# Attention sums from unnormalised exponentials, scaled once per head pair, with prob turned by transposes

## The chip, the cores and the metric

The kernel runs on one core of a Trainium2 chip. Its time is the device time of one execution in microseconds; here there is one core, so it is that core's. Times of single instructions come from one profiled execution.

## The reference, cut to what matters

Two layers, each of a gated feed-forward block, a mixer of three kinds of heads, and another feed-forward block, on 512 tokens of width 1024, all in float32. The change is in the softmax attention of the mixer: 4 heads with shared keys and values (A) and 6 heads whose three dilated windows act as one softmax with a bias added to the scores (B).

```python
def dense_gqa(q, k, v):
    ...
        s = jnp.einsum('bqhgd,bkhd->bhgqk', qi, k).astype(F32) * (D ** -0.5)
        p = jax.nn.softmax(s, axis=-1)
        return jnp.einsum('bhgqk,bkhd->bqhgd', p.astype(v.dtype), v)

def dilated_branch(q, k, v, rel_bias, window, dil):
    ...
    lse = jax.nn.logsumexp(s, axis=-1)
    p = jnp.exp(s - lse[..., None])
    o = jnp.einsum('brnhqk,brnkhd->brnqhd', p.astype(v.dtype), vw)
    ...
```

What is needed of a head is softmax(scores) times v: the exponentials weighted with v, divided by the sum of the exponentials of that query row.

## The kernel before, in words

Activations are kept with features on the 128 partitions and the 512 tokens along the free axis. Large matmuls are made in three products of rounded parts (`mm3`, lines 216 to 218). `body` runs, for each of two layers, `ffn`, `mixer`, `ffn`.

Within `mixer` the attention stage is `Mixer.attention` (line 919), a generator of 20 units: 5 head pairs (`tile_`, 0 and 1 are the A heads, 2 to 4 the B heads) times 4 blocks `t` of 128 query tokens. Between units `mixer` puts the other work of the stage: joining the blocks of a triangular solve (lines 699 and 705, fed by DMAs of X and Y), eight steps of a scan over chunks (`delta_scan`, lines 733 to 780, at the units in `SCAN_AT`), and its end (`delta_finish`, line 1028). After the stage, `project_out` multiplies the eight tiles of `self.mix` with the output weights, tile 4, the last head pair, last (`OUT_ORDER`).

A unit has two halves. `scores` makes the scores of the two heads of the pair (TensorE, lines 954 and 955, into `psc`), their row maximum (VectorE, line 962, or line 966 with the bias), the exponential `prob` with its row sum (ScalarE, lines 963 and 968, the sum through `accum_out`), then on VectorE the reciprocal of the sum (line 970) and `share`, the identity scaled row by row with it (line 971). `weigh`, one unit later (`AHEAD = 1`), turns each 128x128 block of prob with a matmul whose right side is `share` (line 981, four to a PSUM bank `ppt`), so that turning and normalising are one matmul; ScalarE copies the bank to SBUF (`pth`, line 984); line 988 multiplies with v and accumulates into `pav`, the lower head in partitions 0 to 63 and the upper in 64 to 127, over four key blocks. At the fourth block, `pav` holds the pair's 512 tokens and is split into `mxh` (ScalarE, line 993) and `mxl` (VectorE, line 994), the two rounded parts that `project_out` reads.

PSUM in this stage: `psc` has two banks (tag s), `ppt` and the blocks of queries and keys that `load` turns (`pqk`, line 887, a transpose with the identity) share two (tag t), and `pav` has one (tag v). The order of the instructions on each engine is made by a planner (`schedule_with_timeline_sim=True`) from its own estimate of times; each engine then runs its list in order.

Of the kernel before, what the change touches and what calls it, by code (L numbers as in the profile page):

```python
# [9 lines left out]
F32 = mybir.dt.float32  # L10
# [3 lines left out]
AF = mybir.ActivationFunctionType  # L14
ALU = mybir.AluOpType
# [4 lines left out]
P = 128  # L20
T = 512
# [3 lines left out]
NT = T // P  # L25
NL = 2
FGROUPS = [8, 7, 7]
AHEAD = 1
# [351 lines left out]
class Mixer:  # L380
# [495 lines left out]
    low, high = slice(0, 64), slice(64, 128)  # L876
# [42 lines left out]
    def attention(self, ap, pp):  # L919
        k, nc, c = self.k, self.nc, self.c  # L920
        ident = c["ident"]
        self.mix, self.exps = [None] * KD, []
        low, high = self.low, self.high
        ops = {0: self.first}

        def load(i):
            bank = lambda: pp.tile([P, T], F32, name="pqk", tag="t", bufs=2)
            home = self.homes[i % 2]
            if i == 1:
                ops[i] = (self.queries(home, self.turned(bank(), self.qkv[0], i), 0.125), *ops[0][1:])  # L930
            elif i < 5:
                g = self.qkv[i - 1]
                ops[i] = (self.queries(home, self.turned(bank(), g, 0), self.gq8),
                          self.keys((i - 1) % 2, self.turned(bank(), g, 1), self.nbk), g[:, :, 256:384])

        state = {}

        def scores(tile_, t):
            ps = [pp.tile([P, T], F32, name="psc", tag="s", bufs=2) for _ in range(2)]
            if t == 0:  # L940
                state["pv"] = pp.tile([P, T], F32, name="pav", tag="v")
                state["bias"] = []
                if tile_ >= 2:
                    for h in (2 * tile_ - 4, 2 * tile_ - 3):
                        bias = ap.tile([P, NWIN], F32, name="bias", bufs=BIAS_BUFS)
                        src = k.line[h:h + 1, 0:P * 2 * T].rearrange("o (p n) -> (o p) n", n=2 * T)
                        nc.sync.dma_start(out=bias, in_=src[:, P - 1:P - 1 + NWIN])
                        state["bias"].append(bias)
            if t == LOAD_AT:
                load(tile_ + 1)  # L950
            tk = slice(t * P, t * P + P)
            q, (kh, kl), v = ops[tile_]
            for par in range(2):
                nc.tensor.matmul(out=ps[par], lhsT=q[par][:, tk], rhs=kh[:, par], start=True, stop=False)
                nc.tensor.matmul(out=ps[par], lhsT=q[par][:, tk], rhs=kl[:, par], start=False, stop=True)
            probs = []
            for par in range(2):
                pb = ap.tile([P, T], F32, name="prob", bufs=2 * AHEAD + 2)
                row = ap.tile([P, 2], F32, name="row", bufs=2 * AHEAD + 2)
                nm, sm = row[:, 0:1], row[:, 1:2]  # L960
                if tile_ < 2:
                    nc.vector.tensor_reduce(out=nm, in_=ps[par], axis=AX, op=ALU.max, negate=True)
                    self.exps.append(nc.scalar.activation(out=pb, in_=ps[par], func=AF.Exp, bias=nm, accum_out=sm))
                else:
                    o = T - P - t * P
                    nc.vector.tensor_tensor_reduce(out=pb, in0=ps[par], in1=state["bias"][par][:, o:o + T], scale=1.0,
                                                   scalar=3e38, op0=ALU.add, op1=ALU.min, accum_out=nm)
                    nc.scalar.activation(out=pb, in_=pb, func=AF.Exp, scale=-1.0, bias=nm, accum_out=sm)
                share = ap.tile([P, P], F32, name="share", bufs=2 * AHEAD + 2)
                nc.vector.reciprocal(out=sm, in_=sm)  # L970
                nc.vector.tensor_scalar(out=share, in0=ident, scalar1=sm, scalar2=None, op0=ALU.mult)
                probs.append((pb, share))
            return probs, state["pv"], v, tile_, t

        def weigh(probs, pv, v, tile_, t):
            tk = slice(t * P, t * P + P)
            turns = []
            for pb, share in probs:
                pt = pp.tile([P, T], F32, name="ppt", tag="t", bufs=2)
                for kt in range(NT):  # L980
                    nc.tensor.matmul(out=pt[:, kt * P:kt * P + P], lhsT=pb[:, kt * P:kt * P + P], rhs=share,  # L981
                                     start=True, stop=True)
                full = ap.tile([P, T], F32, name="pth", bufs=4)
                nc.scalar.activation(out=full, in_=pt, func=AF.Copy)
                turns.append(full)
            for kt in range(NT):
                for hb, full in zip((low, high), turns):
                    nc.tensor.matmul(out=pv[hb, tk], lhsT=v[:, kt, hb], rhs=full[:, kt * P:kt * P + P],  # L988
                                     start=kt == 0, stop=kt == NT - 1)
            if t == NT - 1:  # L990
                hi = k.xp.tile([P, T], F32R, name="mxh", tag=f"xh{tile_}")
                lo = k.xp.tile([P, T], F32R, name="mxl", tag=f"xl{tile_}")
                nc.scalar.activation(out=hi, in_=pv, func=AF.Copy)
                nc.vector.tensor_tensor(out=lo, in0=pv, in1=hi, op=ALU.subtract)
                self.mix[tile_] = hi, lo

        pending = []
        for unit in range(5 * NT):
            pending.append(scores(*divmod(unit, NT)))
            if len(pending) > AHEAD:  # L1000
                weigh(*pending.pop(0))
            yield unit
        for u in pending:
            weigh(*u)
# [136 lines left out]
```

## Time and profile before

| | |
|---|---|
| median of 3 runs | 2210.26 us (2210.14 to 2210.66) |
| profiled execution | 2210.73 us, of which the span of the trace is 2208.9 us |
| TensorE matmul busy | 2174.3 us, 98% |
| VectorE busy | 1130.1 us, 51% |
| ScalarE busy | 782.1 us, 35% |
| line 981, matmuls | 640 records, mean 284 ns, busy 91.8 us |
| line 988, matmuls | 640 records, mean 285 ns, busy 59.2 us |

PE stands for TensorE, PEld for its weight loads, DVE for VectorE, ACT for ScalarE, POOL for GpSimd. Matmuls are pipelined: one lasts about 275 ns from start to end, but the next starts long before that, so busy times of TensorE overlap and what a matmul costs is read from how soon the next one starts, or from the chain of waits, where each piece begins where the one before it ends. The attention stage lies at about 561 to 695 us in layer 0 and 1655 to 1790 us in layer 1.

### The profile page before, as it was taken

The numbers are of one execution on the slowest core, as the hardware profiler recorded it, in microseconds if no ns is written. First come the engines' busy times: TensorE is split into PE (matmuls) and PEld (weight loads), VectorE is DVE, ScalarE is ACT, GpSimd is POOL, SyncE is SP. The second block draws the span as 40 slices with busy tenths as digits, with TensorE's granted clock in tenths as the row PEclk, the third lists the DMA queues.
The fourth block names the chain that finished last, engine by engine and source line by source line (L and its number), as shares of the span: only waits on it lengthen the run. The fifth ranks groups of instructions, "written<-read, shape, count | busy, mean of one in ns | idle before, by whom it ended". The sixth has DMA issues, their size and how long they took to land.

```text
span 2208.9 us, 31208 instructions
## 1 busy us (share of the span) xinstructions
PE 2174.3 (98%) x12868; PEld 1754.8 (79%) x12868; DVE 1130.1 (51%) x1867; ACT 782.1 (35%) x1147; POOL 320.0 (14%) x298
## 2 busy tenths in 40 slices
PE   7999999999999999999999999999999999999999
PEld 5888887779787888888788888877797878888887
DVE  5333344688776543433443333447796755333343
ACT  4222223534754322222332222235446534222221
POOL 3101012120111210101211010123001121101010
PEclk9999999999999999999999999999999999999999
DMA  5432323233302223232323323232322032332323
GB/s 174 128 96 95 96 93 114 92 83 93 85 28 96 94 91 94 95 96 95 89 93 95 96 92 99 90 122 77 93 88 72 28 115 86 96 96 93 98 93 98
DMA packets 93526, 206.88 MB, mean 94 GB/s; under 512 B 38625, under 2 KB 39137, under 8 KB 93384
## 3 DMA queue, kind: packets, MB, share of 16 engines
q1 hardware_dynamic: 91616, 199.98, 29.3%
q10 hardware_dynamic: 1768, 4.91, 0.8%
q8 instruction: 101, 1.65, 0.3%
q14 instruction: 41, 0.34, 0.0%
HBM read 193.83 MB, written 14.18 MB: 94 GB/s over the span
## 4 chain that ended last, share of the span: by engine, by line
PE 91%; DVE 3%; ACT 2%; DMA 2%; issue 1%; POOL 1%; SPq 0%; ACTq 0%; POOLq 0%; DVEq 0%
PE pg L218 15%; PE pg L216 15%; PE pg L217 15%; PE pd L218 7%; PE pd L216 7%; PE pd L217 7%; PE ppt L981 4%; PE pav L988 2%; PE pgr L807 2%; PE pgr L808 2%; PE pgr L806 2%; PE pc L216 1%; PE pc L218 1%; PE pc L217 1%; PE pwo L218 1%; PE pwo L216 1%
## 5 line engine op out<-in xcount | busy, mean ns | idle before, releaser
L210 ACT ACTIVATE whi<-wraw 128x1024 fp32r<-128x1024 f32 (+3 forms) x344 | 351.0, 1022 | 1224.4 <-PE pg L217 659.8
L216 PE MATMUL pg<-xh,whi 128*128 128x512 f32 x1408 | 558.0, 397 | 8.2 <-ACT xh L236 8.1
L217 PE MATMUL pg<-xl,whi 128*128 128x512 f32 x1408 | 558.4, 397 | 2.3 <-DVE xl L237 2.3
L218 PE MATMUL pg<-xh,wlo 128*128 128x512 f32 x1408 | 557.8, 396 | 0.8 <-DVE wlo L211 0.8
L211 DVE TENSOR_TENSOR wlo<-wraw,whi 128x1024 fp32r<-128x1024 f32 (+3 forms) x344 | 408.0, 1186 | 72.5 <-ACT whi L210 63.6
L216 PEld LDWEIGHTS pg<-xh,whi 128*128 128x128 f32 x1408 | 265.2, 188 | 73.0 <-ACT xh L236 8.1
L217 PEld LDWEIGHTS pg<-xl,whi 128*128 128x128 f32 x1408 | 265.1, 188 | 68.0 <-DVE xl L237 4.7
L296 POOL TENSOR_TENSOR s<-s,rstd 128x512 f32<-128x512 f32 x88 | 152.2, 1731 | 1147.1 <-ACT s L295 1147.1
L218 PEld LDWEIGHTS pg<-xh,wlo 128*128 128x128 f32 x1408 | 265.2, 188 | 65.2 <-DVE wlo L211 1.9
L218 PE MATMUL pd<-hh,wlo 128*128 128x512 f32 x704 | 278.8, 396 | 0.9 <-DVE wlo L211 0.9
L216 PE MATMUL pd<-hh,whi 128*128 128x512 f32 x704 | 278.5, 396 | 0.0
L217 PE MATMUL pd<-hl,whi 128*128 128x512 f32 x704 | 278.4, 395 | 0.0
L310 DVE SCALAR_TENSOR_TENSOR x<-pd,x 128x512 f32<-128x512 f32 x96 | 66.4, 691 | 284.7 <-PE pd L218 284.7
L298 DVE TENSOR_TENSOR h<-pg,s 128x512 f32<-128x512 f32 x88 | 60.9, 692 | 288.0 <-PE pg L218 281.5
L294 DVE TENSOR_TENSOR s<-pg,rstd 128x512 f32<-128x512 f32 x88 | 60.6, 691 | 230.5 <-PE pg L218 230.4
L218 PEld LDWEIGHTS pd<-hh,wlo 128*128 128x128 f32 x704 | 132.3, 188 | 34.0 <-DVE wlo L211 2.2
L217 PEld LDWEIGHTS pd<-hl,whi 128*128 128x128 f32 x704 | 132.4, 188 | 31.9
L216 PEld LDWEIGHTS pd<-hh,whi 128*128 128x128 f32 x704 | 132.4, 188 | 31.7
L981 PE MATMUL ppt<-share,prob 128*128 128x128 f32 x640 | 91.8, 284 | 3.8 <-DVE qs L897 3.8
L981 PEld LDWEIGHTS ppt<-share,prob 128*128 128x128 f32 x640 | 80.1, 191 | 15.3 <-issue 5.8
L807 PE MATMUL pgr<-wlo,xh 128*128 128x384 f32 (+1 forms) x256 | 90.1, 352 | 0.2
L808 PE MATMUL pgr<-whi,xl 128*128 128x384 f32 (+1 forms) x256 | 90.0, 353 | 0.0
(248 smaller groups left out, 2506.4 us busy)
## 6 DMA issues: line engine op xcount, KB each, us to landing
wraw<-in_gu_dram SPq DMA_DIRECT2D x176, 512.0 KB, 3.6
wraw<-in_wd_dram SPq DMA_DIRECT2D x64, 448.0 KB, 3.3
wraw<-in_wd_dram SPq DMA_DIRECT2D x32, 512.0 KB, 3.6
wraw<-in_w_c_dram SPq DMA_DIRECT2D x24, 512.0 KB, 3.7
wraw<-in_w_gb_dram SPq DMA_DIRECT2D x24, 384.0 KB, 3.0
wraw<-in_w_o_dram SPq DMA_DIRECT2D x14, 512.0 KB, 4.4
bias<-line SPq DMA_DIRECT2D x12, 448.0 KB, 5.4
saved<-x SPq DMA_DIRECT2D x16, 256.0 KB, 2.0
```

Source lines behind the costliest of these rows:

```text
L210: nc.scalar.activation(out=hi, in_=raw, func=AF.Copy)
L211: nc.vector.tensor_tensor(out=lo, in0=raw, in1=hi, op=ALU.subtract)
L216: nc.tensor.matmul(out=out, lhsT=w[0], rhs=x[0], start=first, stop=False)
L217: nc.tensor.matmul(out=out, lhsT=w[0], rhs=x[1], start=False, stop=False)
L218: nc.tensor.matmul(out=out, lhsT=w[1], rhs=x[0], start=False, stop=last)
L294: nc.vector.tensor_tensor(out=s, in0=p, in1=n["rstd"], op=ALU.mult)
L296: nc.gpsimd.tensor_tensor(out=s, in0=s, in1=n["rstd"], op=ALU.mult)
L298: nc.vector.tensor_tensor(out=h, in0=pp[1], in1=s, op=ALU.mult)
L310: nc.vector.scalar_tensor_tensor(out=self.x[dm], in0=p, scalar=0.5, in1=self.x[dm], op0=ALU.mult, op1=ALU.add)
L807: nc.tensor.matmul(out=o, lhsT=xh[:, tk], rhs=lo[:, wc], start=False, stop=False)
L808: mm = nc.tensor.matmul(out=o, lhsT=xl[:, tk], rhs=hi[:, wc], start=False, stop=kk == KD - 1)
L981: nc.tensor.matmul(out=pt[:, kt * P:kt * P + P], lhsT=pb[:, kt * P:kt * P + P], rhs=share, start=True, stop=True)
```

## The change

The exponentials are no longer normalised before they are weighted. Each row's sum goes into a column of a new tile `sums` (one per head pair, 4 blocks by 2 heads); the reciprocal and the scaled identity of each unit are gone. Line 981's matmul becomes a transpose with the identity, as line 887 has it. At the fourth block of a head pair one reciprocal is taken of all eight columns, and eight matmuls spread it: each multiplies one column, repeated 64 times as the left side, with the identity, which gives 64 equal rows of 128 tokens; the lower head's into partitions 0 to 63 and the upper head's into 64 to 127 of a bank of tag t. ScalarE copies that bank to SBUF (`share`, now 128x512), VectorE multiplies `pav` with it in place, and the split into `mxh` and `mxl` reads the product from SBUF instead of `pav`.

```diff
--- before.py
+++ after.py
@@ -939,6 +939,7 @@
             ps = [pp.tile([P, T], F32, name="psc", tag="s", bufs=2) for _ in range(2)]
             if t == 0:
                 state["pv"] = pp.tile([P, T], F32, name="pav", tag="v")
+                state["sums"] = ap.tile([P, NT, 2], F32, name="sums", bufs=2)
                 state["bias"] = []
                 if tile_ >= 2:
                     for h in (2 * tile_ - 4, 2 * tile_ - 3):
@@ -956,8 +957,8 @@
             probs = []
             for par in range(2):
                 pb = ap.tile([P, T], F32, name="prob", bufs=2 * AHEAD + 2)
-                row = ap.tile([P, 2], F32, name="row", bufs=2 * AHEAD + 2)
-                nm, sm = row[:, 0:1], row[:, 1:2]
+                nm = ap.tile([P, 1], F32, name="row", bufs=2 * AHEAD + 2)
+                sm = state["sums"][:, t, par:par + 1]
                 if tile_ < 2:
                     nc.vector.tensor_reduce(out=nm, in_=ps[par], axis=AX, op=ALU.max, negate=True)
                     self.exps.append(nc.scalar.activation(out=pb, in_=ps[par], func=AF.Exp, bias=nm, accum_out=sm))
@@ -966,20 +967,16 @@
                     nc.vector.tensor_tensor_reduce(out=pb, in0=ps[par], in1=state["bias"][par][:, o:o + T], scale=1.0,
                                                    scalar=3e38, op0=ALU.add, op1=ALU.min, accum_out=nm)
                     nc.scalar.activation(out=pb, in_=pb, func=AF.Exp, scale=-1.0, bias=nm, accum_out=sm)
-                share = ap.tile([P, P], F32, name="share", bufs=2 * AHEAD + 2)
-                nc.vector.reciprocal(out=sm, in_=sm)
-                nc.vector.tensor_scalar(out=share, in0=ident, scalar1=sm, scalar2=None, op0=ALU.mult)
-                probs.append((pb, share))
-            return probs, state["pv"], v, tile_, t
-
-        def weigh(probs, pv, v, tile_, t):
+                probs.append(pb)
+            return probs, state["pv"], state["sums"], v, tile_, t
+
+        def weigh(probs, pv, sums, v, tile_, t):
             tk = slice(t * P, t * P + P)
             turns = []
-            for pb, share in probs:
+            for pb in probs:
                 pt = pp.tile([P, T], F32, name="ppt", tag="t", bufs=2)
                 for kt in range(NT):
-                    nc.tensor.matmul(out=pt[:, kt * P:kt * P + P], lhsT=pb[:, kt * P:kt * P + P], rhs=share,
-                                     start=True, stop=True)
+                    nc.tensor.transpose(out=pt[:, kt * P:kt * P + P], in_=pb[:, kt * P:kt * P + P], identity=ident)
                 full = ap.tile([P, T], F32, name="pth", bufs=4)
                 nc.scalar.activation(out=full, in_=pt, func=AF.Copy)
                 turns.append(full)
@@ -990,8 +987,17 @@
             if t == NT - 1:
                 hi = k.xp.tile([P, T], F32R, name="mxh", tag=f"xh{tile_}")
                 lo = k.xp.tile([P, T], F32R, name="mxl", tag=f"xl{tile_}")
-                nc.scalar.activation(out=hi, in_=pv, func=AF.Copy)
-                nc.vector.tensor_tensor(out=lo, in0=pv, in1=hi, op=ALU.subtract)
+                nc.vector.reciprocal(out=sums, in_=sums)
+                spread = pp.tile([P, T], F32, name="pshare", tag="t", bufs=2)
+                for u in range(NT):
+                    for par, hb in enumerate((low, high)):
+                        nc.tensor.matmul(out=spread[hb, u * P:u * P + P], lhsT=sums[:, u, par:par + 1].to_broadcast([P, 64]),
+                                         rhs=ident, start=True, stop=True)
+                share = ap.tile([P, T], F32, name="share")
+                nc.scalar.activation(out=share, in_=spread, func=AF.Copy)
+                nc.vector.tensor_tensor(out=share, in0=pv, in1=share, op=ALU.mult)
+                nc.scalar.activation(out=hi, in_=share, func=AF.Copy)
+                nc.vector.tensor_tensor(out=lo, in0=share, in1=hi, op=ALU.subtract)
                 self.mix[tile_] = hi, lo
 
         pending = []
```

## Rows read from the trace of the kernel before

**Rows 1.** The page: span; busy time by engine; the chain that ended last, by line

```profile
span 2208.9 us, 31208 instructions
PE 2174.3 (98%) x12868; PEld 1754.8 (79%) x12868; DVE 1130.1 (51%) x1867; ACT 782.1 (35%) x1147; POOL 320.0 (14%) x298
...
PE pg L218 15%; PE pg L216 15%; PE pg L217 15%; PE pd L218 7%; PE pd L216 7%; PE pd L217 7%; PE ppt L981 4%; PE pav L988 2%; PE pgr L807 2%; PE pgr L808 2%; PE pgr L806 2%; PE pc L216 1%; PE pc L218 1%; PE pc L217 1%; PE pwo L218 1%; PE pwo L216 1%
```

**Rows 2.** Stretch: us; busy us of PE, PEld, DVE, ACT, POOL; clock, DMA, GB/s

```profile
600.00:640.00 40.00, 39.23 (x631) 32.42 (x631) 31.69 (x77) 24.16 (x47) 2.83 (x4) 1.00 0.08 25
```

**Rows 3.** Chain of waits, 600 to 640 us (start us, us, what, records)

```profile
by line: PE ppt L981 33.6%; PE pav L988 18.2%; PE prr L746 8.4%; PE psc L954 8.4%; PE pkq L733 6.4%; PE psc L955 6.2%; PE pS L756 6.2%; PE po L769 5.5%; PE pqk L887 2.9%; DVE qs L897 1.9%; ACT qs L896 1.7%; issue 0.5%
...
608.09 1.09 PE ppt L981 x8
...
612.14 0.89 PE ppt L981 x8
...
619.51 1.02 PE pav L988 x14
620.52 0.86 PE ppt L981 x6
...
622.25 0.64 PE ppt L981 x4
622.89 0.36 PE pav L988 x2
623.25 0.58 PE pqk L887 x4
```

**Rows 4.** Groups by line and form (xcount, busy us, mean ns, idle before)

```profile
L981 PE MATMUL ppt<-share,prob 128*128 128x128 f32 x640 | 91.8, 284 | 3.8 <-DVE qs L897 3.8
...
L887 PE MATMUL pqk<-consts,qkv 128*128 128x128 f32 x56 | 10.4, 299 | 0.0
...
L971 DVE TENSOR_SCALAR share<-consts,row 128x128 f32<-128x128 f32 x80 | 28.0, 350 | 1.9
...
L970 DVE RECIPROCAL row<-row 128x1 f32<-128x1 f32 x80 | 12.7, 159 | 16.3 <-ACT prob L963 7.8 <-ACT prob L968 7.0
```

**Rows 5.** Busy time by stretch, line 981 alone (matmuls, weight loads)

```profile
600.00:640.00 40.00, 14.87 (x102) 12.82 (x102) 1.00 0.08 25
```

**Rows 6.** Chain of waits, 640 to 693 us

```profile
681.05 1.02 PE pav L988 x16
...
689.36 0.44 PE pot L1028 x4
```

**Rows 7.** Timeline at two head pairs' ends (start us, us, instruction, idle before, releaser)

```profile
614.27 1.09 PE L988 MATMUL pav<-pth,qkv 128*64 128x128 f32 x14
...
620.56 0.60 ACT L993 ACTIVATE mxh<-pav 128x512 fp32r<-128x512 f32 x1 [1.45 <-PE pav L988]
...
621.19 0.69 DVE L994 TENSOR_TENSOR mxl<-pav,mxh 128x512 fp32r<-128x512 f32 x1 [0.18 <-ACT mxh L993]
...
675.41 0.60 ACT L993 ACTIVATE mxh<-pav 128x512 fp32r<-128x512 f32 x1 [0.98 <-PE pav L988]
...
678.15 0.68 DVE L994 TENSOR_TENSOR mxl<-pav,mxh 128x512 fp32r<-128x512 f32 x1
```

**Rows 8.** Timeline at the last head pair of layer 0

```profile
695.86 0.68 DVE L994 TENSOR_TENSOR mxl<-pav,mxh 128x512 fp32r<-128x512 f32 x1
...
697.95 0.39 PE L216 MATMUL pwo<-mxh,wohi 128*128 128x512 f32 x1
```

**Rows 9.** Timeline at the start of the attention stage of layer 0

```profile
569.25 0.50 PE L954 MATMUL psc<-kh,qs 128*128 128x512 f32 x1 [2.15 <-ACT prob L963]
...
570.97 1.65 PEld L699 LDWEIGHTS pp<-X,Y 32*32 32x32 f32 x100 [0.27 <-DMA X<-s]
...
572.68 1.77 PE L988 MATMUL pav<-pth,qkv 128*64 128x128 f32 x14
```

**Rows 10.** Busy time by stretch, one us (columns as in rows 2)

```profile
571.00:572.00 1.00, 1.00 (x67) 1.00 (x70) 1.00 (x3) 1.00 (x3) 0.00 (x0) 0.50 0.01 4
```

## Prediction

> **What bounds the kernel now.** I read the page first. TensorE is busy for 2174.3 of the 2208.9 us, and of the chain that ended last 4% is line 981, the turning of prob; nothing but TensorE's lines stands high in it [rows 1]. A busy share says little where matmuls overlap, so I then read the stretch that the change touches, the attention stage (about 561 to 695 us, and again about 1655 to 1790 us). Between 600 and 640 us TensorE is busy 39.23 of 40 us, VectorE 31.69, ScalarE 24.16, at a granted clock of 1.00 [rows 2]. Third, the chain of waits of that stretch, whose pieces follow one another on TensorE: its summary gives 33.6% to line 981, 18.2% to the weighted sums of line 988, and to VectorE and ScalarE less than 2% each [rows 3]. So the stage is as long as its TensorE work. What is taken from that work shortens it, until something else is late.
>
> **Turning prob.** The old turning is a matmul of float32 by float32; the new one is a transpose. The groups by line show that the first leaves two records for each call: 4 blocks x 2 heads x 20 units x 2 layers are 320 calls and line 981 has 640 records, while line 887, a transpose of the same 128x128 float32 block, has 56 records for its 56 calls [rows 4]. Price before: 33.6% of the 40 us [rows 3] are 13.4 us, for 102 records [rows 5], which are 12.75 banks of eight: 1.05 us a bank, and single pieces run from 0.89 to 1.09 [rows 3]. Price after: the pieces with four transposes take 0.58 (line 887) [rows 3] and 0.44 us (line 1028) [rows 6]; they stand amid the same neighbours, and I take 0.52 us, between them. Each bank saves 0.53 us, and there are 2 x 20 x 2 = 80 banks: 42.4 us. The ends: 0.89 - 0.58 = 0.31 (25 us) and 1.09 - 0.44 = 0.65 (52 us).
>
> **The reciprocal and the scaled identity.** 80 of each leave VectorE: 12.7 + 28.0 us [rows 4]. They are beside TensorE's work, so I book nothing for them. Between the exponential and the turning the unit loses about 0.16 + 0.29 us of latency, a possible small gain that stays in the range.
>
> **The new work per head pair**, 10 times. (a) The spread: eight matmuls of 128x64 weights by 128 columns, float32, two records each, alternating between the upper and lower rows as line 988 does. Nothing in the stage does just this; sixteen records of line 988 in one piece take 1.02 us [rows 6], and as two and fourteen 0.36 + 1.02 = 1.38 [rows 3]. Sixteen records at line 981's closest spacing (0.89 us for eight) would be 1.78. I take 1.02, the nearest kind in one block: 10.2 us of TensorE, up to 17.8. (b) One small reciprocal, one ScalarE copy out of PSUM (0.60 us, as line 993), one VectorE product (0.69, as line 994) [rows 7]. They lie beside TensorE's work, unless TensorE waits for them, which is the next point.
>
> **Where pv's bank is held longer.** pv has one bank. Before, it is free after the copy and the subtraction, 0.60 + 0.69 us [rows 7]; after, once spread, copy and product are done. The next pair's weighted sums queue behind that on TensorE, in order, and everything behind them. In the tightest boundary the sums end at 619.51 + 1.02 = 620.53 and the next begin at 622.89 [rows 3]: a gap of 2.36 us, filled with ten records of line 981 and a step of the scan. With transposes for ten records (minus 0.66) and the spread (plus 1.02) the same gap holds 2.72 us of work; the new chain wants 1.02 + 0.60 + 0.69 and about 0.2 of handoffs, 2.5 us. So it just fits, if nobody queues. But the spread also takes one of the two banks that the transposes use, and VectorE can be late: at 675 us the subtraction began at 678.15, though its copy from 675.41 took 0.60 [rows 7], 2.1 us in VectorE's queue. I book 0.5 us for each of the 8 inner boundaries: 4.0 us (from 0 to 2 each).
>
> **The last pair of a layer.** The pair's bytes are ready at 695.86 + 0.68 = 696.54, and they are used first at 697.95 [rows 8]: 1.4 us of slack. The new chain adds the spread 1.02, copy 0.60 and product 0.69, 2.3 us and handoffs, on queues that also hold the next weights. I book 1.3 us a layer, 2.6 in all (0 to 6).
>
> **Banks that save nothing.** At the stage's start TensorE waits: 2.15 us for an exponential before 569.25, and at 570.97 for the blocks X that a DMA brings [rows 9]. Two banks in each layer lie ahead of that landing; their 0.53 us turns into waiting. 4 x 0.53 = 2.1 us.
>
> **The sum.** 42.4 - 10.2 - 4.0 - 2.6 - 2.1 = 23.5 us. The profiled execution took 2210.73 us (span 2208.9, 1.8 around it), 0.5 over the median of the runs. 2210.7 - 23.5 - 0.5 = 2186.7: I say 2187. Its own range, from sums with single terms at their bounds, is 2180 to 2196.
>
> **The rivals.**
> The waits are covered. The boundaries and ends cost nothing (all 6.6 us come back) and the shorter path from exponential to turning gives a little more: 32 to 35 us, 2177. For it: the gap above fits by 0.2 us.
>
> Half of it is given back. VectorE keeps 31.69 - 12.75 x 0.51 (a reciprocal and a scaling for each bank [rows 4]) + 1.6 x 0.85 (a head pair's end comes 1.6 times in the stretch) = 26.6 us, while the stretch shrinks from 40 to 34.9: 76%; ScalarE has 25 of 34.9, 72%, where it had 60% [rows 2]. In-order engines that full make TensorE wait. Five us of new waits a layer give 10 back: 2197, up to 2204.
>
> Slower: the boundary becomes the bound. If the order puts the next sums right behind the spread, TensorE waits for copy and product, 1.5 us with handoffs, plus a queue like the 2.1 us seen, plus one ScalarE instruction ahead, 0.7: 4.3 us. Eight of them are 34 us, where 4 are booked: 2217. It decides from about 3.5 us a boundary. Against it: in the trace the four gaps of a layer hold 2.4 us of other work at the least.
>
> [...]
> [...]
>
> No gain: the new call could cost what line 981 does. Then only the added terms are left, 17 us: 2227. Against it stand the 56 records for 56 calls [rows 4].
>
> **How the numbers follow.** Forecast 0.62; covered waits 0.16; half given back 0.14, of which 0.02 ends within 0.2% of before; boundary 0.04; clock 0.02; no gain 0.02. About 0.2% (4.4 us) is what a measurement of this kernel can tell from no change. Faster by more: 0.62 + 0.16 + 0.12 = 0.90; same 0.02; slower 0.08. For 8 in 10 the range reaches from 2174 (covered waits, cheapest transposes) to 2203 (most of the second rival).
>
> **What the profile after would show.** Right: line 981's successor with 320 records, about 0.5 us a bank on the chain; two lines less on VectorE; sixteen records of the spread within 1.0 to 1.4 us; TensorE still over 95% busy between 600 and 670 us, and the output projection starting some 11 us earlier in each layer. Wrong: weighted sums at a head pair's start that wait for the product on VectorE; idle TensorE ahead of transposes whose releaser is the exponential or a copy; a clock under 1.00 in the stage; the first output tile waiting for the last pair. It would also be wrong if a transpose of prob, fresh from ScalarE, took longer than the neighbours' did.

## The result and the profile after

The changed kernel takes 2192.31 us (median of 4 runs, 2189.64 to 2196.07), the kernel before beside it 2210.46 us (4 runs, 2210.14 to 2214.43). The ratio is 0.9915, 95% interval 0.9900 to 0.9930: 18.2 us less. The forecast was 2187 us with 2174 to 2203 as its range. The profiled execution is the fastest of the four, 2189.64 us at a mean granted clock of 0.999; it is 21.1 us under the profiled execution of before in both time and span.

The page of the changed kernel (it answers to [rows 1]): span, busy time by engine, chain by engine.

```profile
span 2187.8 us, 30760 instructions
PE 2138.9 (98%) x12708; PEld 1717.8 (79%) x12708; DVE 1104.2 (50%) x1727; ACT 784.4 (36%) x1157; POOL 320.1 (15%) x298
PE 88%; DVE 4%; DMA 2%; ACT 2%; issue 1%; POOL 1%; SPq 0%; ACTq 0%; DVEq 0%; POOLq 0%
```

Both TensorE's busy time and the span have fallen, TensorE's more (35.4 against 21.1 us): 14 us of it did not arrive. The next two views are the groups by line and form of the changed kernel, turning (L979) and spread (L994): count, then least, median and longest ns. They answer to [rows 4].

```profile
L979 PE MATMUL ppt<-consts,prob x320: 270/273/329, 565.1 to 1763.0; 128*128 128x128 f32 x160
L994 PE MATMUL pshare<-consts,sums x160: 272/273/323, 587.4 to 1765.1; 128*64 128x128 f32 x160
```

Half as many records turn the same blocks (320 for 640), and a record is as long as it was (median 273 ns, 275 before). The chain of waits of the changed kernel from 600 us on (start us, us, what, records), beside [rows 3]:

```profile
605.97 0.59 PE ppt L979 x4
606.56 0.86 PE pkq L733 x48
607.42 0.59 PE ppt L979 x4
...
612.38 0.25 PE pav L985
612.64 0.10 PE pav L985
612.74 0.87 PE pshare L994 x15
613.61 0.43 PE psc L955
...
617.50 0.57 DVE otok L776
618.09 0.69 DVE share L998
618.78 0.60 DVE prob L967
619.39 0.60 DVE prob L967
620.00 1.09 DVE mxl L1000
621.09 0.48 DVE t L736
...
624.17 0.48 DVE vn L749
...
626.13 1.02 PE ppt L979 x8
```

In these pieces a bank of four transposes is 0.51 to 0.59 us, where eight records took 0.89 to 1.09. Every spread stands as one or two pieces of about 0.9 to 1.2 us. New is the piece in the middle: for 7.7 us, from 616.94 to 624.65, the chain runs through VectorE's queue, which works off the new product L998, two tiles of scores and the pair's remainder L1000 before it comes to the scan's next step; TensorE itself stood idle for 1.3 us of that (the row of `pS` below), so the chain says what came last there, not that TensorE lost 7.7 us. In the chain of before no line of VectorE has 2% of that stretch [rows 3].

The waits of TensorE from 561 to 700 us (engine, line, what it waited for: us in all, times, longest), first before, then after, each with its longest rows:

```profile
PE psc L954 <- ACT prob L963: 3.9, 2, 2.1
PE ppt L981 <- DVE qs L897: 1.9, 2, 1.1
PE pwo L216 <- ACT mxh L1033: 0.8, 1, 0.8
```

```profile
PE pav L985 <- ACT pth L981: 3.0, 1, 3.0
PE psc L955 <- ACT prob L964: 1.8, 1, 1.8
PE pot L1034 <- DVE z L1038: 1.6, 2, 1.3
PE psc L955 <- DVE row L967: 1.5, 1, 1.5
PE pS L756 <- DVE vn L749: 1.3, 1, 1.3
...
PE ppt L979 <- ACT share L997: 0.7, 1, 0.7
```

All rows added, they are 7.1 us before and 14.2 after. Only the 0.7 us behind `share` is a wait for the new chain from sums to product; the others stand on copies, exponentials, maxima and scan steps that were there already and were covered. By stretch (us; busy us of PE, PEld, DVE, ACT, POOL; clock, DMA share, GB/s), as [rows 2]:

```profile
600.00:640.00 40.00, 38.24 (x717) 31.24 (x718) 30.00 (x65) 25.55 (x54) 5.79 (x7) 1.00 0.11 37
640.00:660.00 20.00, 17.46 (x331) 13.60 (x330) 14.60 (x31) 13.03 (x25) 5.39 (x6) 1.00 0.02 5
660.00:700.00 40.00, 37.13 (x292) 27.89 (x291) 24.79 (x64) 19.71 (x39) 4.33 (x8) 1.00 0.30 106
```

TensorE is 95.6% busy up to 640 us (98.1% before, [rows 2]) and 87% in the 20 us behind that.

For the comparisons below I cut each layer's attention stage in three by its records: start (first scores to the last matmul that joins the blocks, line 705), middle (to the last weighted sum), end (to the first tile of the output projection added to x, on VectorE). Times in us, layer 0 / layer 1; "waits" adds up, over the whole stage, what the start-to-start times of TensorE's records over 0.36 us have above 0.22 us, a rough split of work and waiting. "Fourth tile" is the time from the first scores to the fourth tile added to x, and "at 0.50" how much of that time TensorE's granted clock was at 0.50.

| kernel (profiled execution) | start | middle | end | stage | waits | fourth tile | at 0.50 |
|---|---|---|---|---|---|---|---|
| before | 26.0 / 27.4 | 107.1 / 107.1 | 4.6 / 4.6 | 137.7 / 139.1 | 8.7 / 10.5 | 155.1 / 156.5 | 3.4 / 3.4 |
| after | 25.6 / 24.3 | 93.9 / 96.8 | 8.7 / 6.5 | 128.2 / 127.7 | 16.8 / 16.2 | 146.0 / 145.1 | 0.0 / 3.4 |

The two stages give 9.5 + 11.4 = 20.9 us, so all of the gain lies in them.

### The profile page after: what moved, and what is told of

Read it like the earlier page. It is cut to its first block, busy times and chain, and to the rows that moved or that the text cites. A ratio compares the mean times of both kernels' runs of the same rounds, so it can differ in the third digit from the quotient of the medians.

```text
span 2187.8 us, 30760 instructions
## 1 busy us (share of the span) xinstructions
PE 2138.9 (98%) x12708; PEld 1717.8 (79%) x12708; DVE 1104.2 (50%) x1727; ACT 784.4 (36%) x1157; POOL 320.1 (15%) x298
## 4 chain that ended last, share of the span: by engine, by line
PE 88%; DVE 4%; DMA 2%; ACT 2%; issue 1%; POOL 1%; SPq 0%; ACTq 0%; DVEq 0%; POOLq 0%
PE pg L218 15%; PE pg L216 15%; PE pg L217 15%; PE pd L218 7%; PE pd L217 7%; PE pd L216 7%; PE pav L985 2%; PE pgr L807 2%; PE pgr L808 2%; PE ppt L979 2%; PE pc L216 2%; PE pc L218 1%; PE pgr L806 1%; PE pc L217 1%; PE pwo L218 1%; PE pwo L216 1%
## 5 line engine op out<-in xcount | busy, mean ns | idle before, releaser
L218 PEld LDWEIGHTS pd<-hh,wlo 128*128 128x128 f32 x704 | 132.3, 188 | 34.0 <-DVE wlo L211 2.2
L217 PEld LDWEIGHTS pd<-hl,whi 128*128 128x128 f32 x704 | 132.4, 188 | 31.9
L216 PEld LDWEIGHTS pd<-hh,whi 128*128 128x128 f32 x704 | 132.4, 188 | 31.8
L807 PE MATMUL pgr<-wlo,xh 128*128 128x384 f32 (+1 forms) x256 | 90.1, 352 | 0.2
L245 POOL TENSOR_TENSOR acc<-acc,sq 128x512 f32<-128x512 f32 x42 | 68.3, 1626 | 132.7 <-ACT sq L244 132.2
L216 PE MATMUL pc<-xh,whi 128*128 128x512 f32 (+1 forms) x208 | 83.6, 404 | 0.8 <-DVE ab L431 0.8
```

The lines of the kernel that those rows point to most:

```text
L216: nc.tensor.matmul(out=out, lhsT=w[0], rhs=x[0], start=first, stop=False)
L217: nc.tensor.matmul(out=out, lhsT=w[0], rhs=x[1], start=False, stop=False)
L218: nc.tensor.matmul(out=out, lhsT=w[1], rhs=x[0], start=False, stop=last)
L245: nc.gpsimd.tensor_tensor(out=n["acc"], in0=n["acc"], in1=sq, op=ALU.add)
L807: nc.tensor.matmul(out=o, lhsT=xh[:, tk], rhs=lo[:, wc], start=False, stop=False)
```

## The experiments

All times are medians of runs on the chip, all ratios against the kernel before on the same chip, where its median was 2210.5 to 2211.8 us. The edits are against the changed kernel unless said otherwise.

| run | us (lowest to highest) | ratio, 95% interval | granted clock |
|---|---|---|---|
| e0_after_again | 2191.1 (2189.3 to 2197.5) | 0.9909, 0.9888 to 0.9930 | 0.993 to 0.997 |
| e1_ident_matmul | 2219.0 (2218.0 to 2220.2) | 1.0031, 1.0020 to 1.0043 | 0.997 to 0.999 |
| e7_one_pass_matmul | 2203.9 (2202.0 to 2206.9) | 0.9962, 0.9948 to 0.9977 | 0.991 to 0.994 |
| e2_no_scaling | 2199.2 (2197.0 to 2201.3) | 0.9939, 0.9924 to 0.9954 | 0.989 to 0.993 |
| e5_pv_freed | 2200.0 (2195.1 to 2203.8) | 0.9942, 0.9921 to 0.9962 | 0.994 to 0.998 |
| e4_spread_transposed | 2206.4 (2201.2 to 2212.6) | 0.9978, 0.9965 to 0.9991 | 0.988 to 0.993 |
| e9_dve_work_back | 2203.6 (2199.1 to 2209.5) | 0.9963, 0.9947 to 0.9979 | 0.991 to 0.995 |
| e10_scan_early | 2194.2 (2188.2 to 2197.1) | 0.9914, 0.9895 to 0.9933 | 0.994 to 0.998 |
| e11_scan_first | 2190.3 (2189.4 to 2195.3) | 0.9909, 0.9892 to 0.9925 | 0.996 to 0.997 |
| e12_spread_tr_first | 2204.4 (2199.5 to 2210.6) | 0.9969, 0.9959 to 0.9978 | 0.990 to 0.995 |
| e13_before_scan_first | 2211.1 (2209.0 to 2213.3) | 0.9997, 0.9988 to 1.0007 | 0.998 |
| e16_scan_uncoupled | 2204.6 (2202.7 to 2211.3) | 0.9974, 0.9962 to 0.9987 | 0.990 to 0.993 |

**Is it the turning?** e1 gives the matmul back and keeps the rest.

```diff
-nc.tensor.transpose(out=pt[:, kt * P:kt * P + P], in_=pb[:, kt * P:kt * P + P], identity=ident)
+nc.tensor.matmul(out=pt[:, kt * P:kt * P + P], lhsT=pb[:, kt * P:kt * P + P], rhs=ident, start=True, stop=True)
```

> The changed kernel, but each block of prob is turned by a float32 matmul with the identity, not by a transpose; sums, spread and scaling stay. Theory 1, the gain is TensorE's time for turning: 80 banks go back from 0.55 to 1.05 us, +40 us on the changed kernel's 2192: about 2232, slower than before by the spread (12.4 us in its trace) and the waits. Theory 2, the gain comes from the shorter way from the exponential to the turning and from VectorE's 41 us less: the time stays near the changed kernel's, 2190 to 2200.

2219.0 us: 26.7 us over the changed kernel, and 7.9 over before (2211.1 on that chip). The groups by line and form of e1 show the second record for each call again:

```profile
L979 PE MATMUL ppt<-consts,prob x640: 270/275/426, 565.2 to 1794.9; 128*128 128x128 f32 x160
```

So the transposes make the gain, and everything else in the change is a cost together, as the sum had it. The cost, some 8 us, is smaller than the 22 us that the expected 2232 would have been, because TensorE's waits went back too: e1 has the spread, the copy and the product as the changed kernel has them, and its two stages hold 20.3 us of waits (table below) where before has 19.2 and the changed kernel 33.0. So the new steps by themselves do not make TensorE wait. The waits come with the shorter turning, or with the order that the planner then makes: a third of TensorE's other records in the stage stand elsewhere in e1, so the run does not part these two.

**Do the transposes cost clock?** e7 turns with one-pass float32r matmuls instead (`prob` written as float32r, an identity of that type, and three small tiles made smaller or joined), one record a block.

```diff
-pb = ap.tile([P, T], F32, name="prob", bufs=2 * AHEAD + 2)
+pb = ap.tile([P, T], F32R, name="prob", bufs=2 * AHEAD + 2)
...
-nc.tensor.transpose(out=pt[:, kt * P:kt * P + P], in_=pb[:, kt * P:kt * P + P], identity=ident)
+nc.tensor.matmul(out=pt[:, kt * P:kt * P + P], lhsT=pb[:, kt * P:kt * P + P], rhs=k.ident_r, start=True, stop=True)
```

> The changed kernel, but prob is rounded to float32r and turned by a one-pass float32r matmul with the identity: four records a bank of the length of a transpose, only no transpose (scores of the B heads are rounded too, so the outputs are less exact). [...] If the price of a bank was the transpose's alone and a one-pass matmul costs more: over 2200.

2203.9 us, the "over 2200" that was expected if the one-pass matmul costs more. Added up from start to next start on TensorE, a record takes 161 ns where the transpose takes 137, or 0.64 us a bank for 0.55: some 8 of the 12 us, part of them at the low clock. The granted clock is 0.991 to 0.994, not higher than the changed kernel's 0.993 to 0.999. So matmuls in the place of the transposes gained no clock, and the changed kernel's profiled execution, with its transposes, has the stage of layer 0 at 1.00 throughout (561.60 to 707.60 us, shown below). That the transposes cost clock is thus not shown; but they stand among matmuls, and no run here has a stretch of transposes alone.

**What do the new steps for each head pair cost?** e2 leaves out reciprocal, spread, copy and product; e5 lets ScalarE copy `pv`, which frees its bank sooner, and VectorE multiply by the spread in PSUM; e4 lets GpSimd repeat the reciprocals and four transposes spread them (12.4 us of TensorE before the edit and 4.4 after it, from start to next start).

```diff
-nc.vector.reciprocal(out=sums, in_=sums)
...
-nc.vector.tensor_tensor(out=share, in0=pv, in1=share, op=ALU.mult)
-nc.scalar.activation(out=hi, in_=share, func=AF.Copy)
-nc.vector.tensor_tensor(out=lo, in0=share, in1=hi, op=ALU.subtract)
+nc.scalar.activation(out=hi, in_=pv, func=AF.Copy)
+nc.vector.tensor_tensor(out=lo, in0=pv, in1=hi, op=ALU.subtract)
```

> The changed kernel without reciprocal, spread and scaling at a head pair's end (pv is split as before the change): the outputs of attention are not divided by their sums. Theory 1, TensorE's work and the wait for pv set the time: the spread's 12.4 us go and the boundary and end waits with them, 12 to 18 us off 2192: 2174 to 2180. Rival, the spread lies in TensorE's waits and its chain costs nothing: 2188 to 2192.

```diff
-nc.scalar.activation(out=share, in_=spread, func=AF.Copy)
-nc.vector.tensor_tensor(out=share, in0=pv, in1=share, op=ALU.mult)
+nc.scalar.activation(out=share, in_=pv, func=AF.Copy)
+nc.vector.tensor_tensor(out=share, in0=spread, in1=share, op=ALU.mult)
```

> The changed kernel, but ScalarE copies pv to SBUF and VectorE multiplies that copy with the spread in PSUM: pv's one bank is free after one copy, as early as before the change, and the bank of the spread is held until the product instead. If the held pv bank costs the 0.5 us for each of 8 boundaries that I booked: 4 us off 2192, 2188. If the new waits are elsewhere (the scan's chain, the layer's end): within 2 us of 2192. If the spread's bank is the scarcer one: slower, 2195.

```diff
-for u in range(NT):
-    for par, hb in enumerate((low, high)):
-        nc.tensor.matmul(out=spread[hb, u * P:u * P + P], lhsT=sums[:, u, par:par + 1].to_broadcast([P, 64]),
-                         rhs=ident, start=True, stop=True)
...
+nc.gpsimd.tensor_copy(out=share.rearrange("p (u e d) -> p u e d", e=2, d=64),
+                      in_=sums.unsqueeze(3).to_broadcast([P, NT, 2, 64]))
+for u in range(NT):
+    nc.tensor.transpose(out=spread[:, u * P:u * P + P], in_=share[:, u * P:u * P + P], identity=ident)
```

> The changed kernel, but GpSimd first repeats the eight reciprocals 64 times along the free axis and four transposes spread them, instead of eight float32 matmuls. Theory 1, TensorE bound: the spread goes from 1.24 us a head pair to 0.55, 7 us off 2192: 2185. Rival, the stage is by now as long as its chains on VectorE and ScalarE: 2190 to 2194; and if the copy on GpSimd is late (over 1 us, behind the scan's own), up to 2197.

None came out faster than the changed kernel. Less work (e2: some 12 us of TensorE) gave 2199.2, a bank freed sooner 2200.0, a cheaper spread 2206.4: each slower than the changed kernel, and slower than every time expected of it. So e5 gives no sign that the held bank of `pv` costs anything. But none of the three varied one thing alone: the planner also moved other instructions, in e2 and e4 about a third of TensorE's records in the stage. The stages:

| kernel (profiled execution) | start | middle | end | stage | waits | fourth tile | at 0.50 |
|---|---|---|---|---|---|---|---|
| e0 | 25.2 / 26.3 | 94.0 / 96.8 | 9.1 / 6.5 | 128.3 / 129.7 | 16.8 / 17.4 | 146.0 / 147.1 | 6.8 / 6.8 |
| e1 | 26.6 / 27.3 | 111.9 / 111.4 | 4.6 / 4.6 | 143.1 / 143.3 | 10.3 / 10.0 | 160.5 / 160.7 | 3.4 / 6.8 |
| e2 | 29.3 / 23.7 | 90.1 / 98.0 | 15.6 / 19.6 | 135.0 / 141.2 | 19.6 / 25.6 | 147.4 / 153.6 | 20.5 / 23.9 |
| e5 | 27.9 / 25.0 | 96.9 / 99.6 | 7.6 / 6.5 | 132.4 / 131.1 | 18.0 / 16.1 | 149.7 / 148.5 | 6.8 / 6.8 |
| e4 | 25.2 / 25.7 | 97.6 / 97.1 | 16.3 / 16.0 | 139.1 / 138.9 | 20.0 / 19.0 | 151.5 / 151.2 | 17.1 / 17.1 |
| e9 | 25.7 / 26.5 | 102.0 / 96.1 | 14.8 / 7.6 | 142.4 / 130.2 | 19.5 / 17.7 | 154.8 / 147.6 | 17.1 / 6.8 |
| e16 | 26.4 / 27.6 | 94.6 / 97.5 | 16.4 / 16.1 | 137.4 / 141.1 | 20.5 / 21.1 | 149.8 / 153.5 | 10.2 / 20.5 |

e2 and e4 have an end of 15 to 20 us where the changed kernel has 6.5 to 9. Not all of that is lost: in e2, e4, e16 and layer 0 of e9 the planner put some 19 matmuls of the projection's later tiles ahead of the first sum with x, so that their end holds 44 records of TensorE and the changed kernel's 21 to 23. The fourth tile, behind which the kernels have done the same projection work up to two matmuls, is the fair mark: it is 5.5 and 6.1 us later in e4 than in the changed kernel, all of the 11.5 us between the two profiled executions. What is late at the end is the finish of the scan, which the output projection needs too. VectorE's rows at the end of layer 0 (start us, us, instruction, idle before and releaser), in the changed kernel:

```profile
678.13 1.02 DVE L1029 TENSOR_TENSOR otok<-otok,orq 128x384 f32<-128x384 f32 x2
681.58 0.69 DVE L998 TENSOR_TENSOR share<-pav,share 128x512 f32<-128x512 f32 x1 [2.43 <-PE pav L985]
682.19 0.74 DVE L1038 SCALAR_TENSOR_TENSOR z<-pot,small,z 128x512 f32<-128x512 f32 x1
682.97 0.69 DVE L1000 TENSOR_TENSOR mxl<-share,mxh 128x512 fp32r<-128x512 f32 x1
```

and in e4:

```profile
684.08 0.69 DVE L998 TENSOR_TENSOR share<-pav,share 128x512 f32<-128x512 f32 x1 [0.32 <-PE pav L985]
...
685.46 0.69 DVE L1000 TENSOR_TENSOR mxl<-share,mxh 128x512 fp32r<-128x512 f32 x1
...
686.88 1.03 DVE L1029 TENSOR_TENSOR otok<-otok,orq 128x384 f32<-128x384 f32 x2
688.65 0.75 DVE L1038 SCALAR_TENSOR_TENSOR z<-pot,small,z 128x512 f32<-128x512 f32 x1 [0.74 <-PE pot L1034]
```

In the changed kernel the scan's last tile (L1029) is done before the last pair's product; in e4 it stands behind it in the same queue, and TensorE waits for it (waits of TensorE, e4, 561 to 700 us):

```profile
PE pot L1034 <- DVE otok L1029: 3.5, 1, 3.5
```

Behind that wait the clock is low too. By stretch (columns as above), e4 at that place:

```profile
684.00:687.00 3.00, 0.00 (x0) 0.00 (x0) 2.68 (x11) 1.69 (x2) 0.00 (x0) 0.97 0.70 274
687.00:693.60 6.60, 5.20 (x17) 3.90 (x18) 5.78 (x8) 2.21 (x3) 0.00 (x0) 0.50 0.28 101
693.60:697.00 3.40, 3.40 (x16) 2.73 (x16) 1.45 (x3) 0.73 (x2) 0.00 (x0) 0.99 0.95 302
```

After three us without TensorE the granted clock is 0.50 for 6.6 us.

**How much of this is one kernel's own spread?** e0 is the changed kernel once more.

> The changed kernel itself, again, beside the next three on one chip. Its four runs so far lay between 2189.6 and 2196.1 at mean granted clocks of 0.999 to 0.994, the higher time at the lower clock. If waits of TensorE now let the clock fall in some executions, the spread and the order of time and clock come back: 2189 to 2197, median 2192. If it was the chip: all within 1 us.

2191.1 us, and the spread came back with the clock: 2189 to 2192 at 0.997, 2197.5 at 0.993. One program shows both cases at one place. TensorE's rows at the start of layer 0, e0:

```profile
564.57 0.75 PE L955 MATMUL psc<-kh,qs 128*128 128x512 f32 x1 [1.78 <-ACT prob L964]
565.12 0.63 PE L956 MATMUL psc<-kl,qs 128*128 128x512 f32 x1
565.54 1.05 PE L979 MATMUL ppt<-consts,prob 128*128 128x128 f32 x4
```

and the execution of the changed kernel shown above:

```profile
564.57 0.50 PE L955 MATMUL psc<-kh,qs 128*128 128x512 f32 x1 [1.79 <-ACT prob L964]
564.91 0.40 PE L956 MATMUL psc<-kl,qs 128*128 128x512 f32 x1
565.15 0.60 PE L979 MATMUL ppt<-consts,prob 128*128 128x128 f32 x4
```

The same wait, 1.78 and 1.79 us, ended at the same microsecond; behind it the clock was 0.50 in one (from 565 to 568 us) and 1.00 in the other. Read at equal clocks, e2 is no slower than the changed kernel (2197.0 and 2197.5 at 0.993), and e4 still is (2203.0 at 0.993). So the low clock is a large part of what the slower kernels lose. Whole stages of layer 0 (in e2 layer 1) by stretch, the changed kernel, e10, which runs the very same instructions in the same order (below), and e2:

```profile
561.60:707.60 146.00, 131.17 (x2053) 101.58 (x2052) 95.27 (x207) 92.09 (x197) 26.44 (x34) 1.00 0.26 77
562.90:713.10 150.20, 135.70 (x2053) 105.02 (x2053) 95.15 (x207) 92.32 (x197) 26.48 (x34) 0.95 0.25 75
1647.90:1801.50 153.60, 134.13 (x1971) 103.00 (x1970) 92.81 (x194) 89.71 (x191) 26.96 (x33) 0.92 0.25 73
```

The runs of one kernel give the price: over all of them a mean clock lower by 0.001 comes with about 1.7 us more, an estimate by a straight line through the runs of each kernel. From the changed kernel's median of 0.997 to the 0.991 of e2, e4 and e7 that is some 10 us, where their medians are 7 to 14 us above the changed kernel's. The runs do not show the clock as a cause beside the waits, though: in the rows above it fell behind them (3.0 us without TensorE in e4, 1.78 us in e0), and no run held it fixed.

**Is VectorE's removed work worth something?** e9 brings the reciprocal and a scaled identity back for every unit, used by nobody.

```diff
+nc.vector.reciprocal(out=row[:, 1:2], in_=sm)
+nc.vector.tensor_scalar(out=k.ones[:, 1:P], in0=ident[:, 1:P], scalar1=row[:, 1:2], scalar2=None, op0=ALU.mult)
```

> The changed kernel with the unit's reciprocal and scaled identity computed as before, but used by nobody: 80 x 0.51 = 41 us back on VectorE, nothing else. My prediction booked their removal at nothing: 2190 to 2195. If VectorE's chains (scan, finish of the scan's heads) are what TensorE now waits for, its 41 us in the stage delay them: 2198 to 2206.

2203.6 us, 11 to 12 more, as the rival had it; at a clock of 0.994 it is 2201.2 to 2205.3, where the changed kernel's order has 2196.0 to 2197.1. But the trace puts nearly all of it in one layer: layer 1 has its fourth tile at 147.6 us, as e0 with 147.1, though VectorE is at 87% there, from 28.9 of 40 us in the changed kernel; by stretch, e9:

```profile
1693.00:1733.00 40.00, 35.81 (x670) 28.70 (x670) 34.66 (x88) 25.59 (x52) 4.03 (x6) 1.00 0.08 25
```

Layer 0 has 154.8 us for 146.0, 8.8 more, with 17.1 us at the low clock for 6.8. So some 20 us of VectorE work cost nothing in one layer and came with 9 us in the other: the work as such need not cost. In both layers about a quarter of TensorE's records stand in another order than in the changed kernel; that the order makes the difference is likely and not shown.

**Is the scan the new bound?** In all kernels the scan's steps are 8 to 12 us apart in most places; two are 14 to 16 us apart in e4. e10 asks for the steps at earlier units, e11 for a higher priority of the scan and its finish in the planner, e12 does that to e4, e13 to the kernel before. e16 cuts the chain of states in e4, with every instruction kept.

```diff
-SCAN_AT = (1, 2, 3, 5, 6, 8, 9, 11)
-FINISH_AT = 12
+SCAN_AT = (1, 2, 3, 4, 5, 6, 7, 8)
+FINISH_AT = 9
```

> The changed kernel with the scan's eight steps issued at units 1 to 8 and its finish at unit 9, instead of 1 to 11 and 12: the same work, earlier. Theory: what was given back is TensorE waiting for the serial chain of scan and finish on VectorE (waits for vn, z and otok in the trace), above all after the last unit: 4 to 8 us off, 2185 to 2188. Rival, the chain is not late, the sum of TensorE's work sets the end: 2190 to 2194. If scan steps closer together make TensorE wait for each of them: 2196 to 2202.

The edit of e11, and the same on e4 (e12) and on the kernel before (e13):

```diff
-for _ in range(SCAN_AT.count(unit)):
-    next(scan)
+with self.tc.high_priority():
+    for _ in range(SCAN_AT.count(unit)):
+        next(scan)
...
-    m.delta_finish(sp)
+    with self.tc.high_priority():
+        m.delta_finish(sp)
```

> The changed kernel with the scan's steps and its finish at high priority in the planner, ahead of attention's work that is ready at the same time. Theory: the scan is a serial chain of about 10 us a step, from 30 us after the stage's start to 104, its finish to 117, and after the change it ends about when attention's last sums do (120), so that both hold the stage. With priority a step takes 7 to 8 us, the finish is done by 100 us, the waits at the layer's end (3.6 and 2.0 us) go, and attention's TensorE work alone sets the end: 3 to 8 us off 2191, 2183 to 2188. Rival, the scan is beside the path and its priority only delays attention: 2191 to 2200.

> The spread by four transposes (label e4, 2206 us) with the scan and its finish at high priority. There the finish ended at 127 us of the stage though the last sums began at 123, and TensorE waited 3.5 us for it, then ran at the low clock. If the late scan is what made that kernel slower than the changed one though TensorE has 7 us less to do: 15 to 20 us off, 2186 to 2191, not slower than the same priority without it. Rival, the copy on GpSimd or the order as a whole is at fault: 2198 to 2206 again.

> The kernel before the change with the scan and its finish at high priority. There attention's last sums begin at 133 us of the stage and the finish is done at 127: the scan has slack. Theory: no gain, 2208 to 2214. Rival, the scan's waits cost TensorE as much there as after: 2202 to 2206.

The edit of e16, on e4:

```diff
+S1 = sp.tile([P, 2, 3, 64], F32, name="S1")
...
-nc.gpsimd.tensor_tensor(out=S, in0=S, in1=self.lstep[:, s].unsqueeze(3).to_broadcast([P, 2, 3, 64]),
+nc.gpsimd.tensor_tensor(out=S1, in0=S, in1=self.lstep[:, s].unsqueeze(3).to_broadcast([P, 2, 3, 64]),
                         op=ALU.mult)
-nc.vector.tensor_tensor(out=S, in0=new, in1=S, op=ALU.add)
+nc.vector.tensor_tensor(out=S1, in0=new, in1=S1, op=ALU.add)
```

> The kernel with the spread by four transposes (e4, 2206.4 us), in which the scan's steps no longer depend on one another: every step reads the state that the first one leaves, and the running state is written beside it and read by nobody. All instructions of the scan stay, on the same engines; what goes is only the chain through the state, so that the output of the scan is not the reference's. Theory 1 (the scan's chain of seven steps and its finish is what ends the stage late in e4: the finish ends 127.0 us after the stage's first scores, the last weighted sums 122.8, and output tiles wait 3.5 us for the finish): without the chain the finish ends before the last sums, the end of the stage shrinks from 16 us to the 6.5 to 8.7 of the changed kernel, and the time falls by 2 x 8 us or more, to 2183 to 2191, so that the 7 us of TensorE work which e4 saves show at last. Theory 2 (the order of the instructions on the queues as a whole is worse there, and the scan is late because of it): the time stays between 2199 and 2208. Between 2192 and 2198: part of each.

None of the five moved its base: 2194.2 and 2190.3 beside 2191 to 2192, 2204.4 and 2204.6 beside 2206.4, 2211.1 beside 2211.7 on that chip. Four of them could not: in the traces every engine of e10 runs the same instructions in the same order as in the changed kernel, every engine of e13 as in the kernel before, and e11 and e12 differ from their bases in the place of one TensorE record. The planner gave the same order again, so these four are further runs of their bases and say nothing about the scan; with them the changed kernel's order has 16 runs, from 2188.2 to 2197.5 us. Only e16 tests something, at e4's order (but for two instructions of GpSimd) with the chain cut. The scan's finish did not come sooner; in e4 the finish ends 127.0 us after the first scores in both layers, in e12 129.6 and 132.3, and in e16, where no step needs the one before, 125.2 and 129.3. The waits of TensorE in e16, 561 to 705 us, have the same row as e4:

```profile
PE pot L1035 <- DVE otok L1030: 3.5, 1, 3.5
```

So theory 1 of the last run falls: the finish is not late for the chain of states. What is left is where its instructions stand among the attention's in queues that run in order, and the finish's own row of small VectorE steps, which stayed; no run parts these. What in the planner's costs and due times moves the instructions with so small an edit as e4's was not found, and no run varied the order alone. No kernel with another order beat the changed one.

## Why the prediction was right, and where it was off

**Turning prob: right.** Count every TensorE record of the two stages from its start to the next start, and take out the waits as the table has them. Then the turning takes 79.9 us before and 37.5 after, 1.00 and 0.47 us a bank: 42.4 us less, as the sum had it. (With the waits behind its records it is 84.3 and 43.7, 1.05 and 0.55 us a bank.) e1 shows it from the other side: 79.2 us for the turning.

**The spread: a little more.** 6.2 + 6.2 us by the same count, 1.24 us a pair, between the 1.02 taken and the 1.78 of the bound: 12.4 us for 10.2. Not booked: the weighted sums take 5.6 us less than before (54.0 to 48.4), which no run explains, and all other lines 1.0 us more.

**Boundaries, ends and start: the amount was too small and the place was in part wrong.** 4.0 + 2.6 + 2.1 = 8.7 us were booked. TensorE's waits grew from 19.2 to 33.0 us in the two stages, 13.8 us. In the start they grew by 3.9 us (2.1 booked), though the start as a whole did not lose: 26.0 and 27.4 us became 25.6 and 24.3. At the ends they grew by 2.6, as booked; the ends are 4.1 and 1.9 us longer because they also hold more records (23 and 21 for 14). The middle has 7.2 us, where the sum had 4.0 for the inner boundaries, but not for their reason: the waits show a single one of 0.7 us for the new chain, in layer 0. So the gap "just fits" was right. The rest of the middle is waits that more TensorE work had covered (scores for their exponential's buffer, weighted sums for a copied block, the scan for VectorE); e1, with the same new chain, the longer turning and another order, does not have them (20.3 us in all).

**The sum against the trace.** 42.4 - 12.4 + 5.6 - 1.0 = 34.6 us less work, less 13.8 of new waits: 20.8 of the 20.9 us. The forecast was 23.5. It is as close as it is in part by luck: the costs of the spread and of the waits were taken 2.2 and 5.1 us too low, and 5.6 us of the weighted sums, which nobody had counted on, made up for most of it; without them the gain would have been some 15 us. The median gained less than the profiled execution (18.2 for 21.1), which was the one with the highest clock.

**VectorE's 41 us booked at nothing: not decided.** Layer 1 of e9 agrees, layer 0 doesn't; that the two come out so differently speaks against VectorE's load as such, but the run can't part it from the order and the clock.

**The rivals.** The likeliest case held in its mechanism, and "half of it is given back" is where the missing 5 us lie: its step (in-order engines make TensorE wait once TensorE has less to do) is what the waits show (33.0 us for 19.2), at 5.1 us beyond those booked and not the 10 that this rival gave. "The boundary" did not come. A slower kernel through the clock, with a chance of 0.02, did not come, and e7, which turns prob without transposes, had the clock lower than the changed kernel (medians 0.991 and 0.997). What came is a low clock behind waits in slower kernels: in e4 0.50 for 6.6 us behind 3.0 us without TensorE. "No gain" is refuted by the 320 records. Of the marks set for the profile after, the records, the bank's time, the spread's time and the earlier projection (9.5 and 11.4 us) came as said; TensorE over 95% busy held to 640 us and not from 640 to 660 (87%). Of the marks of being wrong, transposes waited for a copy once (0.7 us), and the clock was under 1.00 for 3.4 us in layer 1, as it was in each layer before.

**What the method missed.** "As long as its TensorE work" was true at 98% busy, but of the net 34.6 us of TensorE work that went three fifths arrived, 20.9 us, and of e2's further 12 us nothing. The working had no term for the order that the planner makes anew after an edit, nor for the clock, which fell to 0.50 behind some of the waits (1.78 us in e0) and not behind others (1.79 us in the other execution), and by e2, e4, e5, e9 and e12 the kernel can come out 7 to 14 us slower than the changed one for edits that take TensorE work away or leave it as it is; that is nearly as large as the change's own gain.

## What to carry to other kernels

Turn float32 blocks by a transpose and not by a float32 matmul with an identity, if an exact scaling can be done later: here it halved the records (640 to 320), and that paid for all that had to be added (42.4 us less turning, 18.2 us less time). When a stage is bound by one engine at 98%, count on a part of a saving only (here 20.9 of 34.6 us), and then search for the waits that the engine's own work had hidden. Where a planner orders the instructions, compare the order of the records before and after an edit: an edit meant to move nothing may move a third of them, and one meant to move them may move none.

## What the runs showed that was not expected

- The same wait of TensorE was followed by the low clock in one execution and not in another: 1.78 us of waiting was followed by 0.50 (565 to 568 us) in e0, 1.79 us at the same place by 1.00 in the other execution; at 0.50 four transposes took 1.05 us, at 1.00 0.60.
- Kernels with less TensorE work in the stage ran at a lower mean clock: 0.988 to 0.993 in e2 and e4, 0.997 to 0.999 in before and e1. At one order of instructions, 3.4 us at 0.50 in the two stages (the changed kernel) and 20.5 us (e10) lay 7.5 us apart in time.
- Four edits to the order that the planner was asked for (e10 to e13) left the order of the instructions as it was.
- The 8 us of spreading saved by e4 came with 14 us more time than the changed kernel has. What its trace shows for it: a last scan tile behind the last pair's product in one queue, 3.5 us of waiting and 6.6 us at a granted clock of 0.50 after it, and 34 us at the low clock in the two stages in all.
